# Weight parts of a hybrid decoder layer that begin at rotating places modulo 256 bytes

## The chip, the core and the metric

The kernel runs on one core of one Trainium2 chip. The metric is device time in microseconds, from a median of timed runs. A profile is one execution recorded by the hardware profiler; its times are counted from its first instruction, and its span is the time from the first to the last instruction. Engines are named as the profile names them: PE is TensorE's matmuls, PEld its weight loads, DVE is VectorE, ACT is ScalarE, POOL is GpSimd, SP the queue that issues most DMAs.

## The reference

One decoder layer on 512 tokens of width 1024, in float32: half a SwiGLU feed-forward step (FFN), a mixing stage with two attention branches, and another half FFN step.

```python
x = x + 0.5 * swiglu_ffn(x, ffn1_norm, ffn1_w_gate, ffn1_w_up, ffn1_w_down)      # D_FF = 2816
h = rms_norm(x, mix_norm)
(fq, fk, fv, ff, dq, dk, dv, iq, ik, iw, ga, gb) = split_columns(h @ w_in)
o_a = fox_attention(rms_norm(fq), rms_norm(fk), fv, log_sigmoid(ff + b_forget))  # 8 heads of 64
o_b = dsa_attention(rms_norm(dq), rms_norm(dk), dv, iq, ik, iw, rel_bias)        # top-128 keys per query
merged = sigmoid(ga) * (o_a @ w_branch_a) + sigmoid(gb) * (o_b @ w_branch_b)
x = x + merged @ w_out
x = x + 0.5 * swiglu_ffn(x, ffn2_norm, ffn2_w_gate, ffn2_w_up, ffn2_w_down)
```

Nearly all of the arithmetic is in the products of activations with weight matrices. What the change touches is only where in SBUF the weights of these products lie.

## The kernel before

Activations are kept with features on the 128 partitions and the 512 tokens along a row. Every float32 product is made of three matmuls in a faster type, `float32r`: each operand is split into a high part (the value rounded to that type) and a low part (the value minus the high part). The helper `mm3` then issues high by high, and the two mixed products, into the same accumulator. In the instruction's terms one operand is stationary (128 columns of it are loaded into the array by a weight load of its own) and the other one streams through with 128 to 512 columns.

Weights come in chunks of up to 128 x 1024 floats. A chunk is loaded by SP into a raw tile, and then split into two tiles, `wh` and `wl`, by `load_w` (the begin, and the mixing stage) or `split_w` (the FFNs). ACT casts the raw chunk to `wh`. For most chunks DVE subtracts to get `wl`. For 18 of them ("adding": 8 in the FFNs and 10 in the mixing stage) ACT writes minus the high part and an accumulating DMA from POOL's queue adds the raw chunk. Each of the two tags has three buffers of 1,088 floats in a row, 64 more than the longest chunk needs. A row of 1,088 floats is 4,352 bytes, which is 17 times 256, so the three buffers begin at the same place modulo 256 bytes.

There are 270 chunks, used in this way:

- FFN, features in the first four blocks of 128 (`plain` steps, gate and up): weights stationary, 8 blocks of 128 x 128 per chunk, 512 columns of `xh`, `xl` streaming.
- FFN, the other 18 blocks, in pairs (`pair_steps`): seven products per pair in place of eight, in the way of Strassen, with weights stationary and 256 columns streaming from combined halves of the activations. These are the tiles `b1`, `b2`, `ta`, `tb` in a pool `halves`, whose first tile is a pad of 8 floats, 32 bytes.
- FFN down-projection (`run_down`): weights stationary, 512 columns of the hidden activations `ah`, `al` streaming; in the last FFN the last output tile is done in two halves of 256 columns.
- Mixing stage, feature-major (`fm_proj`; accumulators `ps_f`, `ps_gb`), the branch and output projections (`ps_bb`, `ps_out`): weights stationary, 512 columns streaming.
- Mixing stage, token-major (`tm_proj`, accumulator `ps_t`): here `xh` and `xl` are stationary and the weights stream, 256 columns (208 in the first unit). For these chunks the parts begin at word 8 of their tile, and for all others at word 0 (L127).

The order of TensorE's instructions is the order in which the code issues them, by hand. In the FFNs a step's chunks are loaded and split one or two steps ahead of it (`look_ahead`). In the mixing stage three chunks are taken at a time, and triples of products are put between the attention's short matmuls by a budget. The order on the other engines comes from a planner. It is not part of the change.

Of the kernel before, what the change touches and what calls it, by code (L numbers as in the profile page):

```python
# [11 lines left out]
F32 = mybir.dt.float32  # L12
F32R = mybir.dt.float32r
AF = mybir.ActivationFunctionType
OP = mybir.AluOpType
# [3 lines left out]
P = 128  # L19
# [32 lines left out]
def tile_hybrid_layer(ctx: ExitStack, tc: tile.TileContext, a: dict):  # L52
    nc = tc.nc
    V, S, G, PE = nc.vector, nc.scalar, nc.gpsimd, nc.tensor
# [4 lines left out]
    wpool = ctx.enter_context(tc.tile_pool(name="wpool", bufs=3))  # L59
# [7 lines left out]
    def tmp_tile(name):  # L67
        return tmp.tile([P, T], F32, tag="t", name=name)
# [37 lines left out]
    def raw_tile(tag):  # L106
        return wpool.tile([P, 1024], F32, tag=tag, bufs=1, name=tag)

    def split_w(raw, f=1024, adding=False):
        wh = wpool.tile([P, 1088], F32R, tag="wh", name="wh")  # L110
        wl = wpool.tile([P, 1088], F32R, tag="wl", name="wl")
        S.copy(wh[:, :f], raw[:, :f])  # L112
        if adding:
            S.mul(wl[:, :f], wh[:, :f].bitcast(F32), -1.0)
            G.dma_start(wl[:, :f], raw[:, :f], accum_op=OP.add)
        else:
            V.tensor_sub(wl[:, :f], raw[:, :f], wh[:, :f].bitcast(F32))  # L117
        return wh[:, :1024], wl[:, :1024]

    def load_w(src, n, m, raw=None, adding=False):  # L120
        f = n * m
        if raw is None:
            raw = raw_tile(next(raw_tags))
        wh = wpool.tile([P, 1088], F32R, tag="wh", name="wh")
        wl = wpool.tile([P, 1088], F32R, tag="wl", name="wl")

        wh, wl = (w[:, at:at + f] for w in (wh, wl) for at in [8 if m > P else 0])  # L127
        with tc.high_priority(offset=1 if first else 30):
            nc.sync.dma_start(raw[:, :f].rearrange("p (n m) -> p n m", n=n), src)
            S.copy(wh, raw[:, :f])  # L130
            if adding:

                S.mul(wl, wh.bitcast(F32), -1.0)
                G.dma_start(wl, raw[:, :f], accum_op=OP.add)
            else:
                V.tensor_sub(wl, raw[:, :f], wh.bitcast(F32))
        return (wh.rearrange("p (n m) -> p n m", n=n),
                wl.rearrange("p (n m) -> p n m", n=n))
# [54 lines left out]
    def ffn(n, nxt, parts=lambda d: [slice(0, T)]):  # L193
        wg, wu, wp, wd = (a[f"w_{nm}{n}"] for nm in ("gate", "up", "pair", "down"))
        gi = 0 if n == 1 else 2
        with tc.tile_pool(name=f"ffn{n}", bufs=1) as ap, tc.tile_pool(name=f"halves{n}", bufs=1) as hp:
# [90 lines left out]
            def plain(src, f, run, adding=False, ahead=2):  # L287
                raw = {}

                def split():  # L290
                    return [t[:, :f * P].rearrange("p (n m) -> p n m", n=f)
                            for t in split_w(raw["a"][0], f * P, adding)]
                return Step(raw, [("a", f, src)], split, run, "a", ahead)

            pg = [None]
# [19 lines left out]
            def pair_steps(q, last):  # L315
# [24 lines left out]
                def split_a():  # L340
                    t["s1"] = stream(0, F32, "s1")
                    V.tensor_add(t["s1"], raw["c"][0], raw["d"][0])
                    return split_w(raw["a"][0])

                def split_s2():
                    t["s2"] = stream(1, F32, "s2")
                    V.tensor_add(t["s2"], t["s1"], raw["a"][0])
                    return split_w(t["s2"])
# [144 lines left out]
    with tc.tile_pool(name="begin", bufs=1) as bp, tc.manual_schedule(  # L493
            engines={mybir.EngineType.SP, mybir.EngineType.Activation, mybir.EngineType.DVE}):
        squares = []
        S.dma_start(x[0], a["x"][:, 0, :])
        for d in range(KD):
            for dst, src, at in zip(first, ("w_gate1", "w_up1"), ({0: (0, 2), 2: (2, 8)}, {1: (0, 4), 4: (4, 8)})):
                if d in at:
                    lo, hi = at[d]  # L500
                    w = load_w(a[src][0][:, lo:hi], hi - lo, P, bp.tile([P, 1024], F32, name=f"raw{d}"))
                    dst += [(w[0][:, k], w[1][:, k]) for k in range(hi - lo)]
            if d:
                nc.sync.dma_start(x[d], a["x"][:, d, :])
            else:
                nc.sync.dma_start(gains, a["gains"])
            prep(d, 0)
            if d > 3:
                squares.append(square(d - 4, bp))
        squares += [square(d, bp) for d in range(4, KD)]  # L510
        for d in range(KD):
            add_square(d, squares[d])
# [7 lines left out]
    with (tc.tile_pool(name="mix", bufs=1) as mp, ExitStack() as att_ctx,  # L520
          tc.tile_pool(name="mix_dram", bufs=1, space=bass.MemoryType.DRAM) as mp_dram):
        at = att_ctx.enter_context(tc.tile_pool(name="att", bufs=1))
# [93 lines left out]
        def weight(src, n, m):  # L616

            me = len(chunks)
            chunks.append([src, n, m, None])

            def take():
                for i, c in enumerate(chunks[me:me + 3], me):
                    if c[3] is None:
                        c[3] = load_w(*c[:3], adding=i in ADDING)
                return chunks[me][3]
            return take
# [220 lines left out]
        for h in range(H):  # L847
# [3 lines left out]
            for i in range(1, NT):  # L851
                n = P * (i + 1)
# [191 lines left out]
        with tc.tile_pool(name="late", bufs=1) as lp:  # L1044
# [7 lines left out]
            gb[6] = lp.tile([P, T], F32, name="gb6")  # L1052
            nc.sync.dma_start(gb[6], kept[:, 4])
            ps = fm_product(load_w(a["w_gb"][7], KD, P), "ps_gb")
            gb.append(lp.tile([P, T], F32, name="gb7"))
            V.tensor_mul(gb[7], ps, rb)
# [4 lines left out]
            for d in range(KD):  # L1061
                wh, wl = load_w(a["w_bb"][d], 4, P)
# [4 lines left out]
                m = tmp_tile("m")  # L1067
# [6 lines left out]
            for d in range(KD):  # L1074
                wh, wl = load_w(a["w_out"][d], KD, P)
# [87 lines left out]
```

## Time and profile before

| | us |
|---|---|
| median of two timed runs | 1091.01 (1090.87 to 1091.14) |
| span of the profiled execution | 1087.8 |
| PE busy | 1071.0 (98%) |
| PEld busy | 963.3 (89%) |
| DVE busy | 791.2 (73%) |
| ACT busy | 570.6 (52%) |
| POOL busy | 197.6 (18%) |

The page gives no time of the profiled execution beside its span, so its own time is taken as the span; the median of the runs is 3.2 us above it. Busy times of matmuls are from the issue of the first column to the modelled end of the last, and neighbours overlap: a matmul of 256 columns is listed with 0.28 us while the next one starts less than half of that later. So the distance between starts, which the timeline shows, tells the rate. "L141" is a line of the kernel; the three matmuls of `mm3` are L141, L142 and L143, and one name of an operand can stand for many tiles, since buffer numbers are left out.

### The profile page before, as it was taken

How to read it: one execution, taken by the hardware profiler on the slowest of the kernel's cores; microseconds unless marked ns; L12 is line 12 of the kernel's file. 1: busy time of each engine (PE TensorE's matmuls, PEld its weight loads, DVE VectorE, ACT ScalarE, POOL GpSimd, SP SyncE). 2: the span in 40 equal slices, each digit the busy share in tenths (PEclk: the TensorE clock that was granted, in tenths of full speed). 3: DMA queues.
4: the chain of work that ended last, by engine and by line, in shares of the span. 5: the costliest groups of instructions: out<-in, count | busy, mean ns of one | idle time of the engine just before them, and what ended most of it. 6: DMA issues, size and time to landing. Idle time of an engine off the chain costs nothing.

```text
span 1087.8 us, 17784 instructions
## 1 busy us (share of the span) xinstructions
PE 1071.0 (98%) x6808; PEld 963.3 (89%) x6808; DVE 791.2 (73%) x1286; ACT 570.6 (52%) x916; POOL 197.6 (18%) x265
## 2 busy tenths in 40 slices
PE   8999999999999999999999999999999999999998
PEld 6889989998998889999878788788889989989997
DVE  5888767856967579976776765954888758766963
ACT  6635533633555676467766656543635624533550
POOL 1100000100000014367786562000100000000000
PEclk9999999999999999999999999999999999999999
DMA  7554433443442258733323321533544442533441
GB/s 225 134 155 124 110 117 116 112 121 104 125 122 83 84 126 185 207 105 99 87 59 105 123 74 49 165 97 97 126 136 131 125 118 93 136 104 110 126 113 72
DMA packets 45444, 127.87 MB, mean 118 GB/s; under 512 B 5544, under 2 KB 5928, under 8 KB 45360
## 3 DMA queue, kind: packets, MB, share of 16 engines
q1 hardware_dynamic: 38880, 110.22, 33.1%
q0 software_dynamic: 6336, 16.26, 8.2%
q8 instruction: 54, 0.88, 0.3%
q10 hardware_dynamic: 144, 0.26, 0.1%
q14 instruction: 30, 0.25, 0.1%
HBM read 104.94 MB, written 3.42 MB: 100 GB/s over the span
## 4 chain that ended last, share of the span: by engine, by line
PE 53%; DVE 5%; ACT 3%; POOL 3%; issue 2%; DMA 0%; DVEq 0%; POOLq 0%; ACTq 0%
PE pd L142 4%; PE pd L143 4%; PE pd L141 4%; PE ps_f L141 3%; PE ps_f L142 3%; PE ps_f L143 3%; PE pB L142 2%; PE pB L141 2%; PE pB L143 2%; PE ps_t L141 2%; PE ps_t L142 2%; PE ps_t L143 2%; PE pC L142 2%; PE pA L142 2%; PE pA L141 2%
## 5 line engine op out<-in xcount | busy, mean ns | idle before, releaser
L142 PE MATMUL pd<-al,wh 128*128 128x512 f32 (+1 forms) x358 | 138.3, 386 | 1.0 <-DVE al L217 1.0
L141 PE MATMUL pd<-ah,wh 128*128 128x512 f32 (+1 forms) x358 | 138.2, 386 | 0.0
L143 PE MATMUL pd<-ah,wl 128*128 128x512 f32 (+1 forms) x358 | 138.0, 386 | 0.0
L215 POOL DMA_DIRECT2D al<-gu x24 | 20.5, 854 | 490.2 <-ACT al L214 490.2
L112 ACT CAST wh<-s 128x1024 fp32r<-128x1024 f32 x54 | 57.0, 1055 | 92.4 <-PE pB L142 45.9
L419 DVE SCALAR_TENSOR_TENSOR x<-pd,x 128x512 f32<-128x512 f32 (+1 forms) x65 | 44.2, 680 | 62.0 <-PE pd L143 61.8
L141 PE MATMUL ps_t<-wh,xh 128*128 128x256 f32 (+1 forms) x288 | 80.7, 280 | 0.0
L142 PEld LDWEIGHTS pd<-al,wh 128*128 128x128 f32 x358 | 67.2, 188 | 15.0 <-DVE al L217 1.7
L142 PE MATMUL ps_t<-wl,xh 128*128 128x256 f32 (+1 forms) x288 | 80.3, 279 | 0.0
L143 PE MATMUL pB<-tbh,wl 128*128 128x256 f32 x288 | 80.3, 279 | 0.0
L141 PE MATMUL pB<-tbh,wh 128*128 128x256 f32 x288 | 80.3, 279 | 0.0
L142 PE MATMUL pB<-tbl,wh 128*128 128x256 f32 x288 | 80.3, 279 | 0.0
L143 PE MATMUL ps_t<-wh,xl 128*128 128x256 f32 (+1 forms) x288 | 80.2, 279 | 0.0
L141 PEld LDWEIGHTS pd<-ah,wh 128*128 128x128 f32 x358 | 67.3, 188 | 13.6 <-ACT ah L212 0.3
L143 PEld LDWEIGHTS pd<-ah,wl 128*128 128x128 f32 x358 | 67.3, 188 | 13.4
L117 DVE TENSOR_TENSOR wl<-s,wh 128x1024 fp32r<-128x1024 f32 x54 | 65.8, 1218 | 4.2 <-ACT wh L112 3.8
L141 PE MATMUL ps_f<-xh,wh 128*128 128x512 f32 x152 | 60.5, 398 | 0.0
L143 PE MATMUL ps_f<-xh,wl 128*128 128x512 f32 x152 | 59.6, 392 | 0.0
L142 PE MATMUL ps_f<-xl,wh 128*128 128x512 f32 x152 | 59.6, 392 | 0.0
L112 ACT CAST wh<-re 128x1024 fp32r<-128x1024 f32 (+2 forms) x30 | 28.5, 951 | 55.4 <-PE pd L142 15.5
L112 ACT CAST wh<-ra 128x1024 fp32r<-128x1024 f32 (+2 forms) x32 | 29.8, 930 | 48.8 <-PE pd L142 18.7
L141 PEld LDWEIGHTS ps_t<-wh,xh 128*128 128x128 f32 x288 | 54.3, 189 | 0.5
(329 smaller groups left out, 3485.9 us busy)
## 6 DMA issues: line engine op xcount, KB each, us to landing
rb<-in_w_pair_dram SPq DMA_DIRECT2D x16, 512.0 KB, 3.7
re<-in_w_pair_dram SPq DMA_DIRECT2D x16, 512.0 KB, 3.7
rc<-in_w_pair_dram SPq DMA_DIRECT2D x14, 512.0 KB, 3.7
ra<-in_w_pair_dram SPq DMA_DIRECT2D x14, 512.0 KB, 3.6
rd<-in_w_pair_dram SPq DMA_DIRECT2D x12, 512.0 KB, 3.7
al<-gu POOLq DMA_DIRECT2D x24, 256.0 KB, 4.0
rd<-in_w_down_dram SPq DMA_DIRECT2D x12, 384.0 KB, 3.1
rc<-in_w_down_dram SPq DMA_DIRECT2D x10, 384.0 KB, 3.3
```

The lines of the kernel that those rows point to most:

```text
L112: S.copy(wh[:, :f], raw[:, :f])
L117: V.tensor_sub(wl[:, :f], raw[:, :f], wh[:, :f].bitcast(F32))
L141: PE.matmul(out, lh, rh, start=start, stop=False, **more)
L142: PE.matmul(out, lh, rl, start=False, stop=False, **more)
L143: PE.matmul(out, ll, rh, start=False, stop=stop, **more)
L215: G.dma_start(l, u, accum_op=OP.add)
L419: V.scalar_tensor_tensor(x[d][:, cols], ps, 0.5, x[d][:, cols], op0=OP.mult, op1=OP.add)
```

## The change

A generator `places` goes through the words 0 to 63 in steps of 29 modulo 64, over and over. A new helper `part_tiles(f)` takes the two tiles of a chunk and returns their views: the high part begins at the next place, the low part 17 words on, modulo 64. Both `load_w` and `split_w` use it, so each of the 270 chunks has its parts at another multiple of 4 bytes modulo 256 than the chunk before it. The fixed word 8 for streamed weights goes with it. The tiles have the same sizes and tags as before, the activations stay where they are, and the instructions and their order in the code are the same.

```diff
+    places = cycle((29 * i) % 64 for i in range(64))
+
+    def part_tiles(f):
+
+        at = next(places)
+        return (wpool.tile([P, 1088], F32R, tag="wh", name="wh")[:, at:at + f],
+                wpool.tile([P, 1088], F32R, tag="wl", name="wl")[:, (at + 17) % 64:(at + 17) % 64 + f])
+
     def split_w(raw, f=1024, adding=False):
-        wh = wpool.tile([P, 1088], F32R, tag="wh", name="wh")
-        wl = wpool.tile([P, 1088], F32R, tag="wl", name="wl")
-        S.copy(wh[:, :f], raw[:, :f])
+        wh, wl = part_tiles(f)
+        S.copy(wh, raw[:, :f])
         if adding:
-            S.mul(wl[:, :f], wh[:, :f].bitcast(F32), -1.0)
-            G.dma_start(wl[:, :f], raw[:, :f], accum_op=OP.add)
+            S.mul(wl, wh.bitcast(F32), -1.0)
+            G.dma_start(wl, raw[:, :f], accum_op=OP.add)
         else:
-            V.tensor_sub(wl[:, :f], raw[:, :f], wh[:, :f].bitcast(F32))
-        return wh[:, :1024], wl[:, :1024]
+            V.tensor_sub(wl, raw[:, :f], wh.bitcast(F32))
+        return wh, wl
 
     def load_w(src, n, m, raw=None, adding=False):
         f = n * m
         if raw is None:
             raw = raw_tile(next(raw_tags))
-        wh = wpool.tile([P, 1088], F32R, tag="wh", name="wh")
-        wl = wpool.tile([P, 1088], F32R, tag="wl", name="wl")
-
-        wh, wl = (w[:, at:at + f] for w in (wh, wl) for at in [8 if m > P else 0])
+        wh, wl = part_tiles(f)
...
-                    return [t[:, :f * P].rearrange("p (n m) -> p n m", n=f)
-                            for t in split_w(raw["a"][0], f * P, adding)]
+                    return [t.rearrange("p (n m) -> p n m", n=f) for t in split_w(raw["a"][0], f * P, adding)]
```

## The prediction

> **What bounds the kernel now.** I read the page first: who is busy, at what clock, and which chain ended last.
>
> ```profile
> span 1087.8 us, 17784 instructions
> PE 1071.0 (98%) x6808; PEld 963.3 (89%) x6808; DVE 791.2 (73%) x1286; ACT 570.6 (52%) x916; POOL 197.6 (18%) x265
> PEclk9999999999999999999999999999999999999999
> PE 53%; DVE 5%; ACT 3%; POOL 3%; issue 2%; DMA 0%; DVEq 0%; POOLq 0%; ACTq 0%
> ```
>
> TensorE works through the whole span at full granted clock. So what counts is the distance from one matmul's start to the next one's: the end moves by the sum of these distances. The busy times of matmuls overlap and can't be added up. I therefore took distances from the timeline (columns: start, duration, engine, line, operation). First a stretch of the FFN's paired products, 256 columns streaming, and its weight loads.
>
> ```profile
> 299.80 0.28 PE L142 MATMUL pC<-b2l,wh 128*128 128x256 f32 x1
> ...
> 300.15 0.28 PE L142 MATMUL pC<-b2l,wh 128*128 128x256 f32 x1
> 300.15 0.19 PEld L143 LDWEIGHTS pC<-b2h,wl 128*128 128x128 f32 x1
> ...
> 301.90 0.28 PE L142 MATMUL pA<-b1l,wh 128*128 128x256 f32 x1
> ```
>
> There are 18 steps from 299.80 to 301.90: 0.1167 us each. The load of the next stationary block begins at 300.15, in the same hundredth as the stream of the current one: each stream shares its time with one load, and both read SBUF. So the two addresses that can meet are the streamed operand's and the *next* stationary block's. The code gives their relation. A weight buffer is 1,088 words, 17 times 256 bytes, so all three buffers of a tag begin alike modulo 256, as laid out, at 96 bytes, like the activation tiles. Blocks inside are 512 or 1,024 bytes apart. The activation halves lie behind a pad of 8 words, 32 bytes further; the 256-wide weights that are themselves streamed start at word 8. So every full 256-wide product has its stream 32 bytes ahead of its load, and every 512-wide one has 0. One place has 256 columns with a distance of 0: the split last down-projection tile.
>
> ```profile
> 1076.63 0.39 PE L143 MATMUL pd<-ah,wl 128*128 128x512 f32 x1
> ...
> 1080.04 0.39 PE L143 MATMUL pd<-ah,wl 128*128 128x512 f32 x1
> ...
> 1080.38 0.28 PE L142 MATMUL pd<-al,wh 128*128 128x256 f32 x1
> ...
> 1083.97 0.28 PE L142 MATMUL pd<-al,wh 128*128 128x256 f32 x1
> ```
>
> 1080.38 to 1083.97 holds 30 steps: 0.1197 us each. The same operation 32 bytes apart took 0.1167. So 3.0 ns (2.6%) go with the relation of the addresses, the one thing that differs. The 512-wide steps ahead of it, 15 from 1076.63 to 1080.04, take 0.2273.
>
> **How far one step can move.** In the mixing stage products are interleaved with short attention matmuls.
>
> ```profile
> 380.21 0.40 PE L141 MATMUL ps_f<-xh,wh 128*128 128x512 f32 x1
> 380.44 0.40 PE L142 MATMUL ps_f<-xl,wh 128*128 128x512 f32 x1
> 380.68 0.39 PE L143 MATMUL ps_f<-xh,wl 128*128 128x512 f32 x1
> 380.90 0.39 PE L141 MATMUL ps_f<-xh,wh 128*128 128x512 f32 x1
> ...
> 382.74 0.40 PE L143 MATMUL ps_f<-xh,wl 128*128 128x512 f32 x1
> ```
>
> 11 steps from 380.21 to 382.74: 0.2300 us, single ones 0.22 to 0.24, with the same distance of 0 between addresses. In the long FFN stretch every step is 0.2273. So a run of equal matmuls settles at one step, and after an interruption wanders around a higher mean. For 256 columns with weights streaming, and for the 208-wide ones, whose four blocks start at four different places:
>
> ```profile
> 480.26 0.28 PE L141 MATMUL ps_t<-wh,xh 128*128 128x256 f32 x1
> ...
> 482.60 0.28 PE L143 MATMUL ps_t<-wh,xl 128*128 128x256 f32 x1
> 361.82 0.28 PE L142 MATMUL ps_t<-wl,xh 128*128 128x208 f32 x1
> ...
> 363.94 0.27 PE L143 MATMUL ps_t<-wh,xl 128*128 128x208 f32 x1
> 378.44 0.29 PE L579 MATMUL ps_ix<-ikh,st 128*128 128x256 f32 x1
> 378.57 0.28 PE L580 MATMUL ps_ix<-ikl,st 128*128 128x256 f32 x1
> ```
>
> 20 steps of 0.1170 at 256 columns; 19 steps of 0.1116 at 208, where a full load must still fit into a shorter stream. The last two rows, 256 columns whose stream and load lie 128 bytes apart, stand 0.13 apart.
>
> **The change part by part.** How many steps it reaches, by groups (one of the three lines of each triple):
>
> ```profile
> L141 PE MATMUL pd<-ah,wh 128*128 128x512 f32 x346 | 134.8, 390 | 0.0
> L141 PE MATMUL pB<-tbh,wh 128*128 128x256 f32 x288 | 80.3, 279 | 0.0
> L141 PE MATMUL ps_t<-wh,xh 128*128 128x256 f32 x256 | 71.9, 281 | 0.0
> L141 PE MATMUL ps_f<-xh,wh 128*128 128x512 f32 x152 | 60.5, 398 | 0.0
> ```
>
> 256 columns: a pair has 7 products of 8 triples, 18 pairs in both FFNs make 1,008 (two of the seven are the 288 of the pB row), so 3,024 matmuls; with 768 of ps_t, 3,792; the 36 of the split tile go beside them. 512 columns: 346 triples of pd, 152 of ps_f on x, 32 on oA, and by the code 128 of gate and up, 64 of ps_out, 32 of ps_bb, 8 of the last gate: 762 triples, 2,286 matmuls. At the steps above that is 3,792 x 0.1167 = 443 and 2,286 x 0.2273 = 520 us, 963 of 1087.8: one nanosecond on every step moves the end by 6.1 us.
>
> *Fixed places become rotating ones.* A chunk's high part starts at word 29i mod 64, its low part 17 words (68 bytes) on. The change takes from the pairs and from ps_t their distance of 32 bytes, and from the 512-wide products their 0; over the 270 chunks each of 64 distances turns up four times. Within each triple the stationary is high, high, low (or the streamed one high, low, high), so the distance also changes twice per triple. I price the 256-wide steps between the two settled rows, 0.1167 and 0.1197, and nearer to the latter, because only one of the 64 distances is the cheap one seen: 0.1187, so 3,792 x 2.0 ns = +7.6 us. For 512 the steady 0.2273 was reached by repeating one relation; I take the unsettled mean 0.2300: 2,286 x 2.7 ns = +6.2 us. Bounds below: 256 columns at the 208-wide 0.1116 (-5.1 ns, -19.3 us) and 512 at 0.22 (-7.3 ns, -16.7 us). Bounds above: 0.124, a little under the 0.13 of the row at 128 bytes, which is one rounded distance (+7.3 ns, +27.7 us), and 0.235, between the unsettled mean and the 0.24 seen (+7.7 ns, +17.6 us).
>
> [...]
>
> *The writers.* ACT's cast, DVE's subtraction and 18 accumulating DMAs now write at those places too.
>
> ```profile
> L130 ACT CAST wh<-ra x21: 602/1051/1057, 345.2 to 720.8; 128x1024 fp32r<-128x1024 f32 x15, 128x512 fp32r<-128x512 f32 x5, 128x832 fp32r<-128x832 f32 x1
> L112 ACT CAST wh<-s x54: 1050/1056/1061, 76.2 to 1043.4; 128x1024 fp32r<-128x1024 f32 x54
> L117 DVE TENSOR_TENSOR wl<-s,wh x54: 1210/1216/1227, 77.3 to 1044.8; 128x1024 fp32r<-128x1024 f32 x54
> wl<-ra POOLq DMA_DIRECT2D x6, 512.0 KB, 5.0
> PE pg L143 <- DVE wl L117: 0.6, 1, 0.6
> PE pu L143 <- DMA wl<-re: 0.4, 1, 0.4
> ```
>
> Casts at word 8 (L130, in part) and at word 0 (L112) both take 1.05 us, so I cost them at nothing. Cover is there: chunks are split two ahead, and two chunks of 24 steps are 2 x 24 x 0.2273 = 10.9 us (5.6 at 256 columns), against 1.06 + 1.22. An adding DMA lands after 5.0 us, and in all TensorE waited 1.0 us for low parts. Were each of the 18 to take 1 us more without cover, +18; I keep 0 to +2. No wait, queue entry or instruction is added or taken, and the order of work stays.
>
> The sum: 1087.8 + 7.6 + 6.2 = 1101.6 in the profiled execution. The median of 1091.01 lies 3.2 us above the span, so 1104.8; I say 1104 (+1.2%).
>
> **The rivals.** *It goes slower by over 2%.* [...] With the upper bounds it is +45, or 1136. [...] Price 1120, chance 0.28. [...]
>
> *Distances hardly matter.* Steps settle at similar values, 32 bytes being no special place: 1088 to 1095, price 1091, chance 0.18. Against it: 0.1197 beside 0.1167.
>
> *It gets faster.* The present places are poor among the 64: distance 0 gave the worse of the two settled steps, and all 512-wide products have it. If these go down by the same 3.0 ns, -6.9 us, 1084; half way to the lower bounds -18, 1073. For it: single steps of 0.22; against it: the 256-wide products lose the cheap distance. Chance 0.10.
>
> **How the numbers follow.** The forecast, 1097 to 1112, has 0.44; the rivals 0.28, 0.18 and 0.10. A measurement of this kernel tells about 2%, 1069 to 1113. Of the faster rival 0.06 lies below that, 0.04 within; so faster 0.06, within 0.44 + 0.18 + 0.04 = 0.66, slower 0.28. The range 1084 to 1128 leaves out most of the faster rival and the upper third of the slower one.
>
> **What would show it.** The timeline of the changed kernel should have steps that are constant inside a chunk's triples but differ from chunk to chunk: pairs averaging 0.1187, pd 0.2300, the clock still full and waits for wl still about 1 us. [...] Casts or subtractions off 1.05 and 1.22 us, or long waits for low parts, would make the prediction wrong at the writers.

## The result and the profile after

The changed kernel took 1105.7 us (median of two runs, 1105.69 to 1105.72) against 1091.01: a ratio of 1.0139, with a 95% interval of 1.011 to 1.0169. It is slower by 1.4%, since the whole interval lies above 1, and inside the predicted range of 1084 to 1128. The page of its profiled execution, with the lines that answer to those of before:

```profile
span 1104.0 us, 17784 instructions
PE 1089.2 (99%) x6808; PEld 970.8 (88%) x6808; DVE 792.8 (72%) x1286; ACT 570.4 (52%) x916; POOL 197.3 (18%) x265
PEclk9999999999999999999999999999999999999999
PE 51%; DVE 6%; ACT 3%; POOL 3%; issue 2%; DMA 1%; SPq 0%; DVEq 0%; POOLq 0%; ACTq 0%
```

The span grew by 16.2 us, with the same number of instructions and a full granted clock in both (1.000). The busy times of DVE, ACT and POOL moved by 1.6 us at most. The casts, the subtractions, the adding DMAs and TensorE's wait for a low part, by line, in the same kernel:

```profile
L119 ACT CAST wh<-s x54: 1048/1052/1058, 76.6 to 1058.7; 128x1024 fp32r<-128x1024 f32 x54
L124 DVE TENSOR_TENSOR wl<-s,wh x54: 1212/1219/1229, 77.7 to 1060.1; 128x1024 fp32r<-128x1024 f32 x54
wl<-ra POOLq DMA_DIRECT2D x6, 512.0 KB, 5.0
wl<-rc POOLq DMA_DIRECT2D x5, 512.0 KB, 6.8
PE pg L147 <- DVE wl L124: 0.6, 1, 0.6
```

Cast and subtraction stand at 1.052 and 1.219 us in the middle, before 1.056 and 1.216. So the time is between the starts of matmuls. Two stretches of the timeline (start, duration, engine, line), one of a down-projection and one of a pair product:

```profile
165.39 0.39 PE L145 MATMUL pd<-ah,wh 128*128 128x512 f32 x1
...
168.16 0.39 PE L145 MATMUL pd<-ah,wh 128*128 128x512 f32 x1
...
173.06 0.28 PE L145 MATMUL pA<-b1h,wh 128*128 128x256 f32 x1
173.18 0.29 PE L146 MATMUL pA<-b1l,wh 128*128 128x256 f32 x1
173.32 0.28 PE L147 MATMUL pA<-b1h,wl 128*128 128x256 f32 x1
...
173.90 0.29 PE L146 MATMUL pA<-b1l,wh 128*128 128x256 f32 x1
174.04 0.28 PE L147 MATMUL pA<-b1h,wl 128*128 128x256 f32 x1
...
174.62 0.29 PE L146 MATMUL pA<-b1l,wh 128*128 128x256 f32 x1
174.76 0.28 PE L147 MATMUL pA<-b1h,wl 128*128 128x256 f32 x1
```

The 12 steps of the first stretch take 0.2308 us each; before it was 0.2273. In the pair product every sixth step is long (from 173.18, 173.90 and 174.62: 0.14 us in the rounded lines, 132 ns in the records), with shorter ones of 113 to 120 ns between: the steps repeat in a pattern of several matmuls. Added up from the starts of all records, class by class, the two profiled executions compare as follows; the 512-wide sums also hold the waits in that class.

| from start to start, us | count | before | after | difference |
|---|---|---|---|---|
| pairs, 256 wide | 3,024 | 352.8 | 358.2 | +5.4 (1.8 ns each) |
| ps_t, 256 wide | 768 | 90.9 | 92.8 | +1.9 (2.5 ns each) |
| 512 wide | 2,286 | 535.0 | 543.9 | +8.9 (3.9 ns each) |
| all other matmuls | 729 | 104.7 | 104.8 | +0.1 |

### The profile page after: what moved, and what is told of

It reads as the page before. It is cut to its first block, busy times and chain, and to the rows that moved or that the text cites. A ratio compares the mean times of both kernels' runs of the same rounds, so it can differ in the third digit from the quotient of the medians.

```text
span 1104.0 us, 17784 instructions
## 1 busy us (share of the span) xinstructions
PE 1089.2 (99%) x6808; PEld 970.8 (88%) x6808; DVE 792.8 (72%) x1286; ACT 570.4 (52%) x916; POOL 197.3 (18%) x265
## 4 chain that ended last, share of the span: by engine, by line
PE 51%; DVE 6%; ACT 3%; POOL 3%; issue 2%; DMA 1%; SPq 0%; DVEq 0%; POOLq 0%; ACTq 0%
PE pd L146 4%; PE pd L147 4%; PE pd L145 4%; PE ps_f L145 3%; PE ps_f L146 3%; PE ps_f L147 3%; PE pB L146 2%; PE pB L147 2%; PE pB L145 2%; PE pC L146 2%; PE pA L146 2%; PE pA L147 2%; PE pC L147 2%; PE pC L145 2%; PE pA L145 2%
## 5 line engine op out<-in xcount | busy, mean ns | idle before, releaser
L146 PEld LDWEIGHTS ps_t<-wl,xh 128*128 128x128 f32 x288 | 54.6, 190 | 0.5
```

Of the source, the lines that this page charges most:

```text
L146: PE.matmul(out, lh, rl, start=False, stop=False, **more)
```

## The experiments

The addresses that I name are those of the programs as laid out; "distance" is from the start of the load to the start of the stream that runs beside it, in words of 4 bytes modulo 64. It was 8 in the pairs and 0 at 512 columns. The ratios in the tables compare with the kernel before as it was timed together with each group of kernels: 1090.11 us for e1 to e4, 1089.76 for e5 to e8, 1090.32 for e9 to e11 and 1090.43 for e12.

**First: what about the rotation costs?** Four kernels test two theories. R: a run of matmuls is slow because the relation of addresses doesn't repeat. D: every distance has a price of its own. The edits are shown against the changed kernel, the times are compared with the kernel before. e1 sets the low part at the high part's place:

```diff
         at = next(places)
+        low = at
...
-                wpool.tile([P, 1088], F32R, tag="wl", name="wl")[:, (at + 17) % 64:(at + 17) % 64 + f])
+                wpool.tile([P, 1088], F32R, tag="wl", name="wl")[:, low:low + f])
```

> High and low part of a chunk begin at the same place; the place still rotates over all 64 from chunk to chunk. Theory R (a run of matmuls settles when one relation of addresses repeats; high and low parts 68 bytes apart keep it from settling, whatever the distance): each chunk settles after some nine steps, about half of the 14.7 us comes back, 1095 to 1100 us, with settled 512-wide steps near 0.227. Theory D (every distance between stream and load has a price of its own, whatever stands before it): the 64 distances are met as often as in the changed kernel, 1104 to 1107 us. [...]

e2 takes the rotation out and leaves the low part 17 words on; `load_w` passes word 8 where the weights stream:

```diff
-    def part_tiles(f):
-        at = next(places)
+    def part_tiles(f, at=0):
+        low = at + 17
...
-        wh, wl = part_tiles(f)
+        wh, wl = part_tiles(f, 8 if m > P else 0)
```

> No rotation: the high parts at the places of the kernel before (word 0, and word 8 where weights stream), the low parts always 17 words on. Theory R: the relation still changes within each triple, so 1102 to 1108 us, as with the rotation. Theory D: two thirds of the loads keep their old distance, so at most a third of the loss, 1091 to 1098 us, unless the one new distance is dear. [...]

e3 rotates in steps of 16 bytes only:

```diff
-    places = cycle((29 * i) % 64 for i in range(64))
+    places = cycle((4 * 29 * i) % 64 for i in range(16))
...
+        low = (at + 20) % 64
```

> As the changed kernel, but all places are multiples of 4 words (16 bytes), and the low part lies 20 words after the high one. [...] Theories R and D: no difference to the changed kernel, 1102 to 1109 us.

e4 sets all parts at word 29:

```diff
-    places = cycle((29 * i) % 64 for i in range(64))
+    places = cycle([29])
...
+        low = at
```

> Every part, high and low, at word 29: one distance for all 512-wide products, one for the pairs, one for streamed weights, all of them new and off 16 bytes. Theory R: it settles as the kernel before does, 1088 to 1096 us. Theory D: the price of these three distances, 1085 to 1115 us, with steps at once at their value after an interruption. [...]

| | median, us | ratio to before, interval | pairs, ns per step | 512 wide, us in all |
|---|---|---|---|---|
| e1 | 1102.42 | 1.0114 (1.0099 to 1.0129) | 117.8 | 544.1 |
| e2 | 1100.95 | 1.0101 (1.0085 to 1.0116) | 117.8 | 543.5 |
| e3 | 1102.22 | 1.0111 (1.0096 to 1.0126) | 117.9 | 542.8 |
| e4 | 1108.18 | 1.0163 (1.0146 to 1.018) | 120.0 | 541.7 |

e3, with all parts on multiples of 16 bytes, kept the loss, as R and D had it: 1102.22 us, at the low end of their 1102 to 1109, with 117.9 ns in the pairs (118.4 in the changed kernel). Theory R missed e1 (1095 to 1100) and falls at e4, which repeats one relation throughout and is the slowest of all; two settled steps of that kernel (21 from 301.81 to 304.33, 0.1200 us each):

```profile
301.81 0.28 PE L147 MATMUL pB<-tbl,wh 128*128 128x256 f32 x1
...
304.33 0.28 PE L147 MATMUL pC<-b2l,wh 128*128 128x256 f32 x1
```

R comes near in one point, e2 (1100.95, a microsecond below its range): where only every third load has a new distance, the other steps suffer too. 12 down-projection steps average 0.2308, though two of three loads have the old distance. In the records of all down-projection steps of e2 without a wait, those with the new distance average 234 ns and the others 230, where all averaged 227 before.

```profile
160.16 0.39 PE L143 MATMUL pd<-ah,wh 128*128 128x512 f32 x1
...
162.93 0.39 PE L143 MATMUL pd<-ah,wh 128*128 128x512 f32 x1
```

Theory D in the form given missed e2 (1091 to 1098) and just missed e1 (1104 to 1107). But e1's timeline showed what D lacked. Within each chunk, steps run into a pattern, and the mean of that pattern mostly goes with the distance. Four chunks of it, the first two pairs at distances of 42 and 31 words, the last two down-projections at 30 words and at 1:

```profile
192.03 0.28 PE L146 MATMUL pA<-b1h,wh 128*128 128x256 f32 x1
...
194.30 0.28 PE L148 MATMUL pA<-b1h,wl 128*128 128x256 f32 x1
...
212.32 0.28 PE L147 MATMUL pA<-b1l,wh 128*128 128x256 f32 x1
...
213.88 0.28 PE L148 MATMUL pA<-b1h,wl 128*128 128x256 f32 x1
...
256.16 0.40 PE L146 MATMUL pd<-ah,wh 128*128 128x512 f32 x1
...
259.89 0.40 PE L147 MATMUL pd<-al,wh 128*128 128x512 f32 x1
260.35 0.39 PE L146 MATMUL pd<-ah,wh 128*128 128x512 f32 x1
...
263.98 0.39 PE L147 MATMUL pd<-al,wh 128*128 128x512 f32 x1
```

20 steps of 0.1135, 13 of 0.1200, 16 of 0.2331 and 16 of 0.2269. Over the 126 pair chunks of e1, the later half of each averaged 113.3 to 123.4 ns, 118.4 in the middle. Chunks at the same place agreed to about 0.1 ns, with two exceptions: one chunk at 13 words stood at 123.4 beside two at 113.3, and one at 4 words at 120.1 beside two at 117.4. 22 chunks stood below 114: distances of 13, 16, 19, 22, 42, 45, 48 and 51 words. Over 63 of the 64 down-projection chunks (one has too few steps without a wait) it was 226.7 to 236.3, 232.9 in the middle. So the kernel before had close to the best step seen at 512 columns (226.9 ns in its down-projections) and a middling one in the pairs (116.7). In the changed kernel, whose distance also changes within each triple, no chunk came below 115.5 and 229.8.

The distance alone isn't all of it, though. e1's three chunks at 8 words, the distance of the kernel before, stood at 117.8 to 117.9, where every chunk of the kernel before stood at 116.7. One of them, 24 steps of 0.1179:

```profile
219.71 0.28 PE L146 MATMUL pB<-tah,wh 128*128 128x256 f32 x1
...
222.54 0.28 PE L146 MATMUL pA<-b2h,wh 128*128 128x256 f32 x1
```

**Second: is it the distance?** Theory S says that the distance alone sets the step. Four kernels without rotation or with less of it. In all of them `part_tiles(f, at)` takes the place, `split_w` has the pairs' place as its default, the `plain` steps pass theirs and `load_w` passes the place of streamed and of other weights. e5 against the kernel before, in which these places (pairs, streamed, all others) are 0, 8 and 0:

```diff
+    def split_w(raw, f=1024, adding=False, at=56):
...
+        wh, wl = part_tiles(f, 48 if m > P else 0)
```

e6 keeps the places 0, 8 and 0 and moves the activation halves; e8 keeps the halves and moves the pairs' weights:

```diff
-            hp.tile([P, 8], F32, name="pad")
+            hp.tile([P, 16], F32, name="pad")
```

```diff
+    def split_w(raw, f=1024, adding=False, at=8):
```

e7 rotates where no place is passed, which is wherever 512 columns stream:

```diff
+        low = at
+        if at is None:
+            at = next(places)
+            low = (at + 17) % 64
...
+        wh, wl = part_tiles(f, 8 if m > P else None)
```

> No rotation, high and low part at the same place; the pairs' weights at word 56, so that the stream lies 16 words (64 bytes) ahead of the load, streamed weights at word 48, all others at word 0 as in the kernel before. Theory S (a run of equal triples settles at a step that the distance alone sets): the settled steps of single chunks in the rotating kernel with equal parts, 113.3 ns at 16 words in the pairs and 113.4 at 48 words in ps_t, hold through the run: 3,024 x -3.4 ns - 768 x 3.5 ns = -13.0 us, about 1077 us. Rival N (the cheap chunks were lucky starts, not a property of the distance): 1088 to 1098 us, with pairs between 116 and 119 ns.

> All weight places as in the kernel before; the pad ahead of the activation halves is 16 floats in place of 8, so the pairs' distance is 16 words by moving the activations and not the weights. Theory S: the same 113.3 ns in the pairs, -10.3 us, 1080 us. Rival P (the place of the weights counts, not its distance to the stream): pairs stay at 116.7 ns, 1088 to 1092 us.

> One part of the change alone: the places rotate, with the low part 17 words on, only for chunks whose products stream 512 columns; the pairs and the streamed weights stay at their places of before. By the traces of the two kernels the 512-wide steps carry 8.9 of the 16.2 us between first and last matmul: 1099 us. If the forecast's share were right (6.2 us): 1096 us; if the writers or the rotation itself cost something: 1104 us and more.

> All places fixed as in the kernel before, but the pairs' weights at word 8, so their distance to the stream is 0. Theory S: 120 ns in every pair step, as in the split last tile of the kernel before: 3,024 x 3.3 ns = +10.0 us, 1100 us. Rival R (any one relation that repeats settles well): 1088 to 1093 us.

| | distance in pairs | median, us | ratio to before, interval | pairs, ns per step | 512 wide, us in all |
|---|---|---|---|---|---|
| e5 | 16 | 1080.71 | 0.9916 (0.9901 to 0.9931) | 113.7 | 535.3 |
| e6 | 16 | 1093.29 | 1.0034 (1.0021 to 1.0047) | 117.8 | 536.3 |
| e7 | 8 | 1098.38 | 1.008 (1.0063 to 1.0096) | 116.7 | 543.5 |
| e8 | 0 | 1100.10 | 1.0094 (1.0079 to 1.0109) | 120.0 | 534.9 |

e7 landed at the share of the 512-wide steps, 1099: they grew by 8.5 us in it, and the pairs kept their 116.7 ns. e8 came to the step that the prediction had read off the split last tile (0.1197): 22 steps of 0.1200 from 301.72 to 304.36.

```profile
301.72 0.28 PE L144 MATMUL pB<-tbh,wl 128*128 128x256 f32 x1
...
304.36 0.28 PE L142 MATMUL pC<-b2h,wh 128*128 128x256 f32 x1
```

e5 came out ahead of the kernel before, by 9 us and not the 13 expected, and e6, with the same distance, did not. Both expectations for e6 missed: neither 113.3 ns nor 116.7, but 22 steps of 0.1177.

```profile
301.77 0.28 PE L143 MATMUL pC<-b2l,wh 128*128 128x256 f32 x1
...
304.36 0.28 PE L144 MATMUL pA<-b1h,wl 128*128 128x256 f32 x1
```

e5's own timeline holds both steps at one and the same pair of places: 22 steps of 0.1132 up to 287.26, and 21 of 0.1176 from 301.83.

```profile
284.77 0.28 PE L143 MATMUL pC<-tal,wh 128*128 128x256 f32 x1
...
287.26 0.28 PE L144 MATMUL pB<-tah,wl 128*128 128x256 f32 x1
...
301.83 0.28 PE L143 MATMUL pB<-tbl,wh 128*128 128x256 f32 x1
...
304.30 0.28 PE L143 MATMUL pC<-tal,wh 128*128 128x256 f32 x1
```

Nine chunks in a row, 291 to 316 us, ran at 117.5 to 117.9 and the other 117 near 113.3. By the layout, each of the nine uses the same buffers, with the same addresses throughout, as five other chunks of e5, and those five stood at 113.2 to 113.7. In ps_t of e5 (distance 48) chunks stood between 113.3 and 120.1, and that class gained 0.5 of the 2.7 us expected (90.4 against 90.9). So one distance can have two steps, and in e5 the matmuls stayed in the dearer one for nine chunks.

**Third: places or ways in.** Theory A says that the place modulo 64 bytes selects the step together with the distance; S now says that the distance alone sets the possible steps and the way into a run picks one. e9 and e11 move stream and load together, e10 tries the other cheap distance.

In the pairs the stream and the load begin, in bytes modulo 256, at 192 and 128 in e9, at 128 and 192 in e10, and at 160 and 128 in e11. e9 and e11 against the kernel before, and e10 against e5:

```diff
-            hp.tile([P, 8], F32, name="pad")
+            hp.tile([P, 24], F32, name="pad")
...
+    def split_w(raw, f=1024, adding=False, at=8):
```

```diff
-            hp.tile([P, 8], F32, name="pad")
+            hp.tile([P, 16], F32, name="pad")
...
+    def split_w(raw, f=1024, adding=False, at=8):
```

```diff
-    def split_w(raw, f=1024, adding=False, at=56):
+    def split_w(raw, f=1024, adding=False, at=24):
```

> A pad of 24 floats ahead of the activation halves, the pairs' weights at word 8, all others as in the kernel before: stream and load of the pairs begin at 192 and 128 bytes modulo 256, 16 words apart, both multiples of 64 bytes as in e5 (128 and 64), where e6 had 160 and 96. Theory A (distance and place modulo 64 bytes together select the settled step): 113.3 ns, about 1080 us. Rival S (the distance alone, with two settled steps of which the way into a run picks one): 113.3 or 117.8 ns, and changes between them from stretch to stretch.

> As e5, but the pairs' weights at word 24, so their load begins at 192 bytes modulo 256 and the stream at 128: 48 words apart, where single chunks of e1 settled at 113.6 ns or less. Theory A: both are multiples of 64 bytes, so 113.3 ns as in e5, 1078 to 1082 us. Rival (16 words ahead is a special distance): pairs at 116 to 120 ns, 1088 to 1100 us.

> A pad of 16 floats and the pairs' weights at word 8: stream and load keep the distance of the kernel before, 8 words, but both lie 32 bytes further, at 160 and 128 bytes modulo 256. Rival S (the distance alone): 116.7 ns as before, 1088 to 1092 us. Theory A (the places count too): another settled step, 113.3, 117.8 or 120 ns, 1080 or 1093 to 1100 us.

| | distance in pairs | median, us | ratio to before, interval | pairs, ns per step |
|---|---|---|---|---|
| e9 | 16 | 1093.99 | 1.0035 (1.0022 to 1.0048) | 117.8 |
| e10 | 48 | 1080.00 | 0.9907 (0.9891 to 0.9924) | 113.4 |
| e11 | 8 | 1091.32 | 1.0011 (1.0001 to 1.0022) | 116.7 |

Theory A falls at e9: both places are multiples of 64 bytes and the step is 117.8, in all 126 chunks to within 0.4 ns. (A's number for e10 came true.) The changes from stretch to stretch that S allowed for didn't show in e9. S holds at e11, where 32 bytes on for both changed nothing in the pairs. One stretch of each (22 steps: 0.1177, 0.1132, 0.1164):

```profile
301.76 0.28 PE L143 MATMUL pC<-b2l,wh 128*128 128x256 f32 x1
...
304.35 0.28 PE L144 MATMUL pA<-b1h,wl 128*128 128x256 f32 x1
```

```profile
301.81 0.28 PE L142 MATMUL pC<-tah,wh 128*128 128x256 f32 x1
...
304.30 0.28 PE L143 MATMUL pC<-tal,wh 128*128 128x256 f32 x1
```

```profile
301.83 0.28 PE L142 MATMUL pA<-b1h,wh 128*128 128x256 f32 x1
...
304.39 0.28 PE L143 MATMUL pA<-b1l,wh 128*128 128x256 f32 x1
```

e10 has the lowest median of the study, though e5 and e12 lie within its interval. Its gain is all in the pairs: 342.9 us against 352.8. At 48 words all 126 chunks were at 113.3 to 113.8. The streamed weights (ps_t) are 48 words apart too in e10, and there nothing was gained: 91.0 us against 90.9.

**Last: does rotating cost anything in itself?** e12 is e10 with the pairs' places rotating over six of the cheap distances.

```diff
+    places = cycle([24, 53, 30, 21, 50, 27])
...
-    def split_w(raw, f=1024, adding=False, at=24):
-        wh, wl = part_tiles(f, at)
+    def split_w(raw, f=1024, adding=False, at=None):
+        wh, wl = part_tiles(f, next(places) if at is None else at)
```

> As e10, but the pairs' weights rotate from chunk to chunk over six places whose distances to the stream (19, 22, 42, 45, 48 and 51 words) all settled near 113.3 ns in e1; high and low part at the same place. Theory S (the distance sets the settled step, and the rotation is harmless): 113.3 to 114 ns in the pairs, 1079 to 1082 us, like e10. Rival T (each change of place costs a chunk its first steps, as after an interruption): some 8 of 24 steps in 126 chunks at 118 in place of 113.3 ns, +4.7 us, 1084 to 1087 us.

It took 1080.74 us, 0.9916 (0.9902 to 0.993), with pairs at 113.4 ns. 45 steps across several chunks, of which the first and the last stand here, average 0.1133:

```profile
304.82 0.28 PE L145 MATMUL pC<-tal,wh 128*128 128x256 f32 x1
...
309.92 0.28 PE L145 MATMUL pA<-b2l,wh 128*128 128x256 f32 x1
```

Theory T (each change of place costs a chunk its first steps) falls: in the pairs, what costs is which distances the rotation brings, not that the places change from chunk to chunk. At 512 columns this was not tried.

## Why the prediction was right, and where not

The time (1104 forecast, 1105.7 measured), the sign and the path were right: the end moved by the sum of start-to-start distances, and nothing came from the writers. The sum of terms was +13.8 us in the span; measured were +16.2. The median then lay 1.7 us above the span where 3.2 had been carried over, which hid most of the difference; that was luck.

*The 256-wide term* was +7.6, measured +7.3 (5.4 and 1.9). The price between the two settled rows held, but not for the reason given: 0.1167 was not the one cheap distance among 64. e1 shows chunks at 0.1133, others at 0.120 and above; the mean lies near 0.118. That cheaper and dearer distances average out to the price taken was luck. That a full load has to fit into the shorter stream of the 208-wide steps was an estimate of mine beside their 0.1116; no run tested it.

*The 512-wide term* was +6.2 and came out at +8.9: 3.9 ns a step in place of 2.7. This is the mis-sized step. e7, which rotates these weights alone, shows it too: +8.5. I had taken the wandering mean of an interrupted run, 0.2300, as the price of a run that doesn't settle. In e1 runs get into patterns of their own, and mostly higher: the middle of the down-projection chunks is 0.2329. In the changed kernel, where the parts are 68 bytes apart, it is 0.2327. The 3.9 ns are a mean of two cases. Steps without a wait went from 226.9 to 232.9 ns in the down-projections (1,038 matmuls), but only from 231.0 to 234.2 in ps_f (552), the group that the row of 0.2300 came from. By that row ps_f had nothing to lose at a price of 0.2300, so the term should have been taken over 1,734 steps, 4.7 us, and would have missed by more.

*The writers* at nothing: right, cast and subtraction moved by 4 and 3 ns. Adding DMAs from one buffer (rc) landed after 6.8 in place of 5.4 us, and no wait of TensorE for them is listed.

*What would show it.* Steps differ from chunk to chunk, as said; they aren't constant within a chunk's triples, but repeat in patterns of several matmuls (in the pair product above every sixth step was 132 ns, between steps of 113 to 120).

*The rivals.* "Distances hardly matter" is refuted by e8, e5 and e10: 120.0, 113.7 and 113.4 ns with nothing else changed in the pairs. Of the kernel's whole time e5 and e10 gained 0.8 and 0.9%. Between the best and the worst fixed distance in the pairs (e10 and e8) lie 6.6 ns of 113.4. No run shows a step that would make the slower rival's 1120: the slowest kernel, e4, took 1108.18 us, 1.6% above the kernel before. The faster rival was wrong for this change, and its place was wrong too: the reserve lay in the pairs, not in the 512-wide products, whose distance of 0 gave 226.9 ns in the down-projections, within 0.2 ns of the lowest chunk of e1.

Not settled: what in the hardware makes the distance count, why a distance has two steps (113.3 and 117.8 ns at 16 words, 116.7 and 117.8 at 8), and what picks one. e5, e6 and e9 show both steps at 16 words and no rule.

## What to carry to other kernels

When TensorE is busy throughout, read the distance between starts in a long run, not the busy time, and compare runs of one shape that differ only in where their operands begin: here it was 3% of the pairs' step and 0.9% of the kernel's time. A rotation over all places, with both parts at the same place, is a quick search, since in e1 chunks at the same place agreed to about 0.1 ns, with two exceptions among 126 in the pairs. It isn't the final measurement: 8 words gave 117.8 ns there and 116.7 when kept. So fix the places at a distance that looks cheap, time that, and look through the whole run for stretches that have got into another step.

## What was not expected

With one distance kept in the pairs, steps came in few values: 113.3, 116.7, 117.8 and 120.0 ns, and at 512 columns often 226.7 or 233.3; three of the first four are 3.3 ns apart, and the last two 6.6. The 24 steps of a chunk in e1 gave more values between 113.3 and 120.2. Chunks below 114 ns in e1 lie at distances three words apart around 16 and 48: 13, 16, 19, 22, and 42, 45, 48, 51. And one stretch of a kernel can run 4% slower than the next with the same kinds of instructions, shapes and addresses (e5: 117.8 and 113.3 ns).
